# Mamba-2 and differential attention trunk: chunk products issued as two column halves, rows scaled by 1/rms once, and a fixed order of instructions up to there

## The chip, the cores and the metric

The kernel runs on one core of one Trainium2 chip. Its time is the device time of one execution in microseconds (us). The core has five engines that run side by side, each with its own queue: TensorE (PE: matmuls and transposes through the array; its weight loads are listed as PEld), VectorE (DVE), ScalarE (ACT), GpSimd (POOL) and SyncE (SP, which issues most DMAs here). Matmul results go to PSUM, eight banks of 128 x 512 float32; everything else lies in SBUF.

## The reference

One sequence of 512 tokens with 1024 features goes through two layers and a last RMSNorm. Layer 0 is a Mamba-2 mixer, layer 1 a differential attention over keys and values that are projected once from the output of layer 0. The change lies almost wholly in layer 0, so only that is shown:

```
h = rms_norm(x, norm_g)                 # x * (1/rms of the row) * gain
zxbcdt = h @ w_in                       # z: 2048, xbc: 4096, dt: 32 columns
xbc = silu(causal_depthwise_conv(xbc, conv_w, conv_b))   # 4 taps along the tokens
dt = softplus(dt_raw + dt_bias); a = -exp(a_log)
# state-space scan in chunks, per group (8) and head (4 a group):
y_diag = einsum("blsgr,bsgrp->blgrp", cb[..., None] * decay, x_c)   # within a chunk
y_off  = einsum("blgn,bgrpn->blgrp", c_c, state) * exp(acs)         # from earlier chunks
y = y_diag + y_off + d_skip * xs
y = gated_group_rms_norm(y, z, gate_norm_g)
x = x + y @ w_out
```

The kernel takes chunks of 128 tokens, so there are four. The 1/rms of a row is one number a token; it commutes with the projection, and so it can be applied to the rows of x, or to the outcome of the projection.

## The kernel before, in words

**Precision.** Every large product is made of three float32r matmuls: both operands are split into a head and a remainder (`hh`/`hl` for rows, `whi`/`wlo` for weights), and `mm3` (line 227) adds head x head, head x remainder and remainder x head into one bank. A head is written by ACT (a copy that rounds), the remainder by DVE (value minus head). The weights come in blocks of 1 MB (`load`, line 122), each split in four or eight pieces by `head` and `rest` (lines 137 and 143), with the norm's gain multiplied in. The small products of the scan are plain float32, which leaves two records of weight load and two of matmul for each product.

**The start (lines 351 to 450).** x is loaded twice: transposed (`xt`, four tiles of two 128-feature slices) and by tokens (`x_tok`). `split_x` makes `hh` and `hl` from the unscaled transposed rows. The gate projection z0 has four banks `pz0`, one for each tile of 128 tokens; its first half uses slices 0 to 3 of the rows, the second half slices 4 to 7. ACT squares `x_tok` to get the row sums, `rsqrt` (line 233) makes 1/rms as a column `r_col`, and `scales` (line 294) turns it into a row: POOL writes four diagonal matrices, a matmul with ones spreads them over the partitions (`aps_r`), and ACT copies the outcome to SBUF as `r_row`. Meanwhile PE makes `ps_dt`, the dt columns, with small weights `dw`. From `ps_dt` come `pre`, the softplus, the cumulated decays `acs`, which go to DRAM and come back spread over partitions for `decays` (line 532).

**Where 1/rms is applied before.** The rows are never scaled. The gate takes `r_col` as the scale of its SiLU (`z_out`, line 344). Each of the 32 outputs of the group projections is multiplied by `r_row` in PSUM in `conv` (line 477) ahead of the four taps. `pre` is multiplied by its part of the row (line 411).

**The dense stream.** `stream_a` (line 521) yields the large projections one after another in the order `z0 g0 g1 z1 g2 g3 z2 g4 o0 g5 z3 g6 g7 o1 o2 o3`: z for the gate, g for a group's B, C and two x tiles, o for the output projection. `ssd(g)` (line 552) is emitted when group g is through. In it, `pyd` (lines 600 to 607) is the product within a chunk: for each of two halves q of the sequence one bank, in it two chunks times four heads, each `dec[:, h, c, :]` (128 x 128, stationary) against `xdt[:, c, h, :]` (128 x 64, moving). DVE then adds the bank to `dx`.

**What sets the order.** The framework's scheduler orders instructions on each engine from a planned timeline, in which earlier emission has precedence. Where `V.on`, `A.on` or `T.on` is true (class `Ordered`, line 43), the instructions of that engine keep the order in which they are written. Before, this holds for DVE and ACT in the first four slices, and for PE, DVE and ACT from the end of the Mamba layer on in parts.

**The end (lines 902 to 1053).** The output projection of the attention runs in pieces (tile t, column half n, heads hs). For tiles 2 and 3, `add_in` (line 941) adds the residual to the bank in PSUM before its last matmuls, `gate_head` (line 850) makes the rows `oh` (head, ACT) and `ol` (remainder, DVE) for those matmuls, and `square_in`, `last_root` and `scale` do the last norm.

Of the kernel before, what the change touches and what calls it, by code (L numbers as in the profile page):

```python
# [61 lines left out]
def trunk(ctx, tc, x, x_t, par, w_dt, w_in, w_out, w_kvqg, w_bo, d_skip, lam_qk, fin_g, out):  # L62
# [59 lines left out]
    def load(i):  # L122

        seg = segs[i]
        src, gains = source(seg)
        nk = 8 if seg[0] in "vkqt" else 4
        w = 2048 // nk
        raw = wp.tile([P, nk, w], F32, tag="raw", name=f"raw{i}", bufs=2)
        fetched[0] += 1

        def split():

            pool, tags = (bp, ("dec", "dec")) if seg == ("o", 3, 1) else (wp, ("whi", "wlo"))
            hi, lo = (pool.tile([P, nk, w], F32R, tag=tag, name=f"{n}{i}", bufs=2) for n, tag in zip(("whi", "wlo"), tags))
            ready[seg] = (hi, lo)

            def head(k):
                if gains:
                    A.activation(hi[:, k, :], raw[:, k, :], AF.Copy, scale=gains[k])
                else:  # L140
                    A.copy(hi[:, k, :], raw[:, k, :])

            def rest(k):
                if gains:
                    V.scalar_tensor_tensor(out=lo[:, k, :], in0=raw[:, k, :], scalar=gains[k],
                                           in1=hi[:, k, :].bitcast(F32), op0=ALU.mult, op1=ALU.subtract)
                else:
                    V.tensor_tensor(out=lo[:, k, :], in0=raw[:, k, :], in1=hi[:, k, :].bitcast(F32), op=ALU.subtract)

            return [(head, rest, k) for k in range(nk)]  # L150

        if i == 0:

            nc.sync.dma_start(raw[:, 0, :], src[:, 0:w])
            for n in range(2):
                nc.sync.dma_start(xt[0][:, 0, n * 256:(n + 1) * 256], x_t[:, 0, n * 256:(n + 1) * 256])
            nc.sync.dma_start(raw[:, 1, :], src[:, w:2 * w])
            nc.sync.dma_start(xt[0][:, 1, :], x_t[:, 1, :])
            for k in range(2, 4):
                nc.sync.dma_start(raw[:, k, :], src[:, k * w:(k + 1) * w])  # L160
                nc.sync.dma_start(xt[1][:, k - 2, :], x_t[:, k, :])
            for i in range(2, 4):
                nc.sync.dma_start(xt[i], x_t[:, 2 * i:2 * i + 2, :])
            nc.sync.dma_start(prc[:], par[:, C_CB:N_PAR])
        else:
            nc.sync.dma_start(raw.rearrange("p k n -> p (k n)"), src)
        return split
# [102 lines left out]
    def run(gen):  # L270
        for _ in gen:
            pass
# [12 lines left out]

    def squares(ss, t, sq=None):
        if sq is None:  # L290
            sq = small.tile([P, D], F32, tag="wide", name=f"sq{t}", bufs=2)
        A.activation(sq, x_tok[:, t, :], AF.Square, accum_out=ss[:, t:t + 1])

    def scales(tag, ss):

        V.tensor_scalar(out=ss, in0=ss, scalar1=ROOT2 / D, scalar2=ROOT2 * EPS, op0=ALU.mult, op1=ALU.add)
        col = res.tile([P, NT], F32, tag="r_col", name=f"{tag}r_col")
        V.tensor_copy(col, rsqrt(ss, NT, "y"))
        w = small.tile([P, NT + 1, P], F32, tag="wide", name=f"{tag}diag", bufs=2)
        GP.memset(w[:, NT], 1.0)  # L300
        for t in range(NT):
            GP.tensor_tensor(out=w[:, t], in0=ident, in1=col[:, t:t + 1].to_broadcast([P, P]), op=ALU.mult)
        ps = long_bank(f"{tag}ps_r")
        T.matmul(ps, lhsT=w[:, NT], rhs=w[:, 0:NT].rearrange("p t n -> p (t n)"), start=True, stop=True)
        row = res.tile([P, S], F32, tag="r_row", name=f"{tag}r_row")
        A.copy(row, ps)
        return col, row

    def turn_rows(tag, t, xn, hh, hl):
# [33 lines left out]

    def z_out(j, t, ps):
        zs = bp2.tile([P, 512], F32, tag="zs", name=f"zs{j}_{t}", bufs=6)
        A.activation(zs, ps, AF.Silu, scale=r_col[:, t:t + 1])
        zt[j, t] = zs


# [10 lines left out]

    begin = small.tile([P, 1], F32, name="begin", bufs=1)
    A.activation(begin, ident[:, 0:1], AF.Copy)
    first = load(0)()
    wh, wl = ready.pop(("z", 0, 0))
    pz0 = [mm_bank(f"pz0_{t}") for t in range(NT)]
    V.on = A.on = True
    for k in range(4):
        lay(first[k])
        for n in (slice(0, 256), slice(256, S)) if k == 0 else (slice(0, S),):
            split_x(k, n)  # L370
    V.on = A.on = False
    for k in range(4):
        for t in range(NT):
            tk = slice(t * P, (t + 1) * P)
            mm3(pz0[t], (hh[:, k, tk], hl[:, k, tk]), (wh[:, k, :], wl[:, k, :]), k == 0, False)
    for k in range(4, KD):
        split_x(k)
    fetch(2)
    for t in range(NT):
        nc.sync.dma_start(x_tok[:, t, :], x[t * P:(t + 1) * P, :])  # L380
    ss = sm.tile([P, NT], F32, name="ass")
    for t in range(NT):
        squares(ss, t)
    r_col, r_row = scales("a", ss)
    V.tensor_scalar(out=sg1, in0=prm[:, C_SG:C_SG + 1], scalar1=0.5 * (1.0 - LAM0), scalar2=None, op0=ALU.mult)
    dtw_raw = sm.tile([P, KD, H], F32, name="dtw_raw")
    nc.sync.dma_start(dtw_raw[:], w_dt)

# [9 lines left out]
    for k in range(KD):  # L398
        w = dw[:, k].rearrange("p a b h -> p (a b h)")
        T.matmul(ps_dt, lhsT=w, rhs=hh[:, k, :], start=k == 0, stop=False)  # L400
        T.matmul(ps_dt, lhsT=w, rhs=hl[:, k, :], start=False, stop=k == KD - 1)

    pre = sm.tile([P, P], F32, name="pre")
    for c in range(NQ):
        sl, hi, lo = (slice(i * H, (i + 1) * H) for i in (c, 0, 1))
        cs = slice(c * P, (c + 1) * P)
        A.copy(pre[sl, :], ps_dt[lo, cs])
        V.tensor_tensor(out=pre[sl, :], in0=ps_dt[hi, cs], in1=pre[sl, :], op=ALU.add)
# [3 lines left out]
    V.tensor_scalar(out=pre, in0=pre, scalar1=prm[:, C_DTB:C_DTB + 1], scalar2=None, op0=ALU.add)  # L412
    e1 = sm.tile([P, P], F32, name="e1")
    A.activation(e1, pre, AF.Abs)
    A.activation(e1, e1, AF.Exp, scale=-1.0)
# [28 lines left out]
    nc.sync.dma_start(dsk[:], d_skip.partition_broadcast(P))  # L444


    w0 = use(("z", 0, 1))
    for t in range(NT):
        run(tok_mm(pz0[t], t, 1, w0))
        z_out(0, t, pz0[t])  # L450
# [20 lines left out]
    def conv(ps, ft, name, bufs):  # L471
        xc = bp2.tile([P, S], F32, tag=f"xc_{name}", name=f"xc{ft}", bufs=bufs)
        at = C_CW - C_CB + 4 * ft
        cw = [prc[:, at + k:at + k + 1] for k in range(4)]

        u = ps
        V.tensor_tensor(out=u, in0=ps, in1=r_row, op=ALU.mult)
        A.activation(xc, u, AF.Identity, scale=cw[3], bias=prc[:, ft:ft + 1])
        for k in (2, 1, 0):
            d = 3 - k  # L480
            V.scalar_tensor_tensor(out=xc[:, d:], in0=u[:, :S - d], scalar=cw[k], in1=xc[:, d:], op0=ALU.mult, op1=ALU.add)
        A.activation(xc, xc, AF.Silu)
        return xc

# [67 lines left out]
    def ssd(g):  # L552
# [349 lines left out]
    def rows():  # L902
        ws = {0: use_b(("c", 2, 0), 1, 2)}
        for t, n, hs in ((0, 0, (4, 5)), (1, 0, (4, 5)), (0, 1, (4, 5)), (1, 1, (4, 5)),
# [214 lines left out]
```

## Time and profile before

| what | value |
|---|---|
| median of 3 runs | 736.55 us (736.23 to 737.25) |
| the profiled execution | 736.51 us |
| its span on the core | 734.7 us |
| mean granted TensorE clock | 0.998 |
| HBM read and written | 68.02 MB and 2.16 MB, 96 GB/s over the span |
| chain that ended last | PE 86%, DVE 6%, ACT 5% |

The span is what the trace covers; the execution's time is 1.8 us longer. In the page, a line of the first part gives an engine's busy time, its share and its instructions; the slices cut the span in 40 equal parts and give the busy share in tenths. A group's row names the tile that is written, the tiles that are read, the shape, the count, the summed busy time and the mean of one in ns. In the wait view a row names who waited for whom, the sum, how often, and the longest. In the timeline a row starts with the start and the length in us. Nearly all lines say L53, since a helper issues them, so they are told apart by the tiles' names.

### The profile page before, as it was taken

What the parts mean: (1) busy time and instruction counts of PE and PEld (TensorE: products, weight loads), DVE (VectorE), ACT (ScalarE), POOL (GpSimd) and SP (SyncE); (2) the same over time, 40 slices, a digit from 0 to 9 for tenths busy, and PEclk for the clock granted to TensorE, in tenths of its full rate; (3) what the DMA queues carried; (4) which work ended last, traced back from release to release, by engine and by line L of the source; (5) the groups of instructions that cost most, each with busy time, mean ns of one, the idle gap of its engine ahead of it and who ended that gap; (6) DMA issues with size and microseconds to landing.
All of it is one profiled execution on the core that took longest, in us unless ns stands there. A gap on an engine that the chain in (4) does not pass through costs nothing.

```text
span 734.7 us, 10327 instructions
## 1 busy us (share of the span) xinstructions
PE 723.1 (98%) x3733; PEld 605.0 (82%) x3733; DVE 530.8 (72%) x1202; ACT 445.3 (61%) x975; POOL 114.8 (16%) x158
## 2 busy tenths in 40 slices
PE   9999999999999999999999999999999999999996
PEld 7788878888887888877888879888898898889874
DVE  5679955798568669469895655666757857785886
ACT  6849672864829356256433258766766766766566
POOL 0117231402233141150110201000000000000002
PEclk9999999999999999999999999999999999999999
DMA  8552313224132233132113220331221131122003
GB/s 314 215 193 97 128 45 116 78 95 172 59 114 65 108 115 116 58 116 102 71 58 114 87 86 8 115 115 58 65 109 57 58 116 58 58 80 93 29 1 114
DMA packets 12914, 70.83 MB, mean 96 GB/s; under 512 B 1728, under 2 KB 2496, under 8 KB 5312
## 3 DMA queue, kind: packets, MB, share of 16 engines
q1 hardware_dynamic: 12576, 69.90, 26.5%
q8 instruction: 29, 0.48, 0.3%
q10 hardware_dynamic: 288, 0.28, 0.1%
q14 instruction: 21, 0.17, 0.1%
HBM read 68.02 MB, written 2.16 MB: 96 GB/s over the span
## 4 chain that ended last, share of the span: by engine, by line
PE 86%; DVE 6%; ACT 5%; issue 1%; DMA 1%; POOL 0%; ACTq 0%; POOLq 0%; SPq 0%
PE pg L53 20%; PE po L53 13%; PE pz L53 10%; PE pt L53 7%; PE pv L53 6%; PE pq L53 6%; PE pk L53 6%; PE pyd L53 4%; PE pb L53 3%; PE sc L53 3%; PE pc L53 2%; DVE wlo L53 2%; ACT L53 1%; PE pyt L53 1%; PE pxt L53 1%
## 5 line engine op out<-in xcount | busy, mean ns | idle before, releaser
L53 DVE SCALAR_TENSOR_TENSOR wlo<-raw,prm,whi 128x512 fp32r<-128x512 f32 (+1 forms) x256 | 151.4, 640 | 49.6 <-ACT whi L53 49.2
L53 ACT ACTIVATE whi<-raw,prm 128x512 fp32r<-128x512 f32 (+1 forms) x256 | 137.1, 609 | 58.5 <-PE pz L53 12.4
L53 PE MATMUL pg<-a_hi,whi 128*128 128x512 f32 x256 | 102.4, 401 | 0.4 <-DVE xc L53 0.4
L53 PE MATMUL pg<-a_hi,wlo 128*128 128x512 f32 x256 | 102.7, 404 | 0.0
L53 PE MATMUL pg<-a_lo,whi 128*128 128x512 f32 x256 | 101.4, 397 | 0.0
L53 DVE SCALAR_TENSOR_TENSOR xc<-pg,prc,xc 128x511 f32<-128x511 f32 (+2 forms) x96 | 70.0, 743 | 4.4 <-ACT xc L53 3.6
L53 PEld LDWEIGHTS pg<-a_hi,whi 128*128 128x128 f32 x256 | 48.2, 188 | 11.4 <-issue 0.8
L53 PEld LDWEIGHTS pg<-a_hi,wlo 128*128 128x128 f32 x256 | 48.1, 188 | 11.0
L53 PEld LDWEIGHTS pg<-a_lo,whi 128*128 128x128 f32 x256 | 48.2, 188 | 10.8
L53 PE MATMUL po<-whi,yh 128*128 128x512 f32 x128 | 50.9, 400 | 0.7 <-ACT yh L53 0.6
L53 PE MATMUL po<-wlo,yh 128*128 128x512 f32 x128 | 50.9, 400 | 0.4 <-DVE wlo L53 0.4
L53 PE MATMUL pz<-wlo,a_hi 128*128 128x512 f32 x128 | 50.5, 401 | 0.0
L53 PE MATMUL pz<-whi,a_lo 128*128 128x512 f32 x128 | 50.1, 399 | 0.0
L53 PE MATMUL po<-whi,yl 128*128 128x512 f32 x128 | 49.9, 396 | 0.0
L53 PE MATMUL pz<-whi,a_hi 128*128 128x512 f32 x128 | 49.6, 400 | 0.0
L53 ACT ACT_TABLE_LOAD x33 | 42.3, 1283 | 9.5 <-DVE xc L53 7.9
L957 POOL TENSOR_TENSOR ot<-ot,fg 128x512 f32<-128x512 f32 x4 | 5.1, 1285 | 257.6 <-PE pc L53 256.4
L53 ACT ACTIVATE s<-s,mx 128x128 f32<-128x128 f32 (+3 forms) x64 | 35.6, 559 | 9.5 <-DVE mx L53 9.3
L580 POOL TENSOR_TENSOR xe<-xdt,tok 128x256 f32<-128x256 f32 x24 | 15.4, 672 | 152.5 <-DVE xdt L53 152.5
L53 DVE CUSTOM_DVE_ANT_0 s<-sc,bias 128x128 f32<-128x128 f32 (+3 forms) x64 | 29.4, 488 | 12.3 <-PE sc L53 11.9
L53 PE MATMUL pv<-whi,b_hi 128*128 128x256 f32 x128 | 36.6, 286 | 0.0
L53 ACT ACTIVATE tmp<-dx 128x256 f32<-128x256 f32 x32 | 13.1, 411 | 38.0 <-DVE dx L53 38.0
(244 smaller groups left out, 1749.1 us busy)
## 6 DMA issues: line engine op xcount, KB each, us to landing
raw<-in_w_in SPq DMA_DIRECT2D x23, 1024.0 KB, 4.9
raw<-in_w_kvqg SPq DMA_DIRECT2D x16, 1024.0 KB, 4.8
dec<-acs_d SPq DMA_DIRECT2D x8, 1024.0 KB, 4.8
raw<-in_w_out SPq DMA_DIRECT2D x8, 1024.0 KB, 4.7
raw<-in_w_bo SPq DMA_DIRECT2D x4, 1024.0 KB, 4.8
x_tok<-in_x SPq DMA_DIRECT2D x4, 512.0 KB, 9.4
out<-ot SPq DMA_DIRECT2D x7, 256.0 KB, 2.4
raw<-in_w_in SPq DMA_DIRECT2D x4, 256.0 KB, 5.4
```

The source lines that it names most:

```text
L53: i = op(*args, **kw)
L580: GP.tensor_tensor(out=xe[:, c], in0=xdt[:, c], in1=toe_tok[:, c, hs].unsqueeze(2).to_broadcast([P, R, HD]), op=ALU.mult)
L957: GP.tensor_tensor(out=o, in0=o, in1=f, op=ALU.mult)
```

## The change

Five things are changed.

1. **Chunk products in halves** (`ssd`). Each `pyd` product becomes two, with columns 0 to 63 and 64 to 127 of `dec` as the stationary side, written to partitions 0 to 63 and 64 to 127 of the bank. The moving side is the same for both.
2. **Rows scaled once.** After the first projection, the row of 1/rms stays in PSUM and DVE multiplies the transposed rows `xt` by it, slice by slice (`scale_x`); ACT and DVE then write `hh` and `hl` anew in place (`head_x`, `rest_x`). z0 still uses `r_col`; the later gates use scale 1. `conv` loses its multiplication and reads the bank directly.
3. **Another `scales`.** The diagonals are written by DVE instead of POOL, the row's matmul is issued by a function that is called later, between the second and the third token tile of the second half of z0, and the copy to SBUF is gone.
4. **A fixed order** on PE, DVE and ACT from the start to the scaled rows. The dt weights are loaded early, in the place of the conv parameters `prc`, which go behind the third weight block; the second and third weight blocks are fetched at fixed places.
5. **Two residual additions at the end.** `add_in(2, 0)` is moved from the stream to behind `gate_head(h, 0, 2)`; `add_in(3, 1)` is moved into `gate_head(h, 3, 4)`, between the head and the remainder.

```diff
@@ load(0)
-            nc.sync.dma_start(prc[:], par[:, C_CB:N_PAR])
+            nc.sync.dma_start(dtw_raw[:], w_dt)
@@ scales
-        V.tensor_copy(col, rsqrt(ss, NT, "y"))
         w = small.tile([P, NT + 1, P], F32, tag="wide", name=f"{tag}diag", bufs=2)
         GP.memset(w[:, NT], 1.0)
+        V.tensor_copy(col, rsqrt(ss, NT, "y"))
         for t in range(NT):
-            GP.tensor_tensor(out=w[:, t], in0=ident, in1=col[:, t:t + 1].to_broadcast([P, P]), op=ALU.mult)
+            V.tensor_scalar(out=w[:, t], in0=ident, scalar1=col[:, t:t + 1], scalar2=None, op0=ALU.mult)
         ps = long_bank(f"{tag}ps_r")
-        T.matmul(ps, lhsT=w[:, NT], rhs=w[:, 0:NT].rearrange("p t n -> p (t n)"), start=True, stop=True)
-        row = res.tile([P, S], F32, tag="r_row", name=f"{tag}r_row")
-        A.copy(row, ps)
+        def row():
+            T.matmul(ps, lhsT=w[:, NT], rhs=w[:, 0:NT].rearrange("p t n -> p (t n)"), start=True, stop=True)
+            return ps
         return col, row
@@ z_out
-        A.activation(zs, ps, AF.Silu, scale=r_col[:, t:t + 1])
+        A.activation(zs, ps, AF.Silu, scale=1.0 if j else r_col[:, t:t + 1])
@@ start
-    V.on = A.on = False
+    T.on = True
...
-    fetch(2)
+    second = load(1)()
     for t in range(NT):
         nc.sync.dma_start(x_tok[:, t, :], x[t * P:(t + 1) * P, :])
-    ss = sm.tile([P, NT], F32, name="ass")
-    for t in range(NT):
-        squares(ss, t)
-    r_col, r_row = scales("a", ss)
...
+    third = load(2)()
+    nc.sync.dma_start(prc[:], par[:, C_CB:N_PAR])
@@ behind ps_dt
+    for piece in second:
+        lay(piece)
+    ss = sm.tile([P, NT], F32, name="ass")
+    for t in range(NT):
+        squares(ss, t)
     pre = sm.tile([P, P], F32, name="pre")
     for c in range(NQ):
...
+        A.copy(pre[c * H:(c + 1) * H, :], ps_dt[H:2 * H, c * P:(c + 1) * P])
+    r_col, row = scales("a", ss)
+    def scale_x(k):
+        V.tensor_tensor(out=xt[k // 2][:, k % 2, :], in0=xt[k // 2][:, k % 2, :], in1=r_row, op=ALU.mult)
+    def head_x(k):
+        A.copy(hh[:, k, :], xt[k // 2][:, k % 2, :])
+    def rest_x(k):
+        V.tensor_tensor(out=hl[:, k, :], in0=xt[k // 2][:, k % 2, :], in1=hh[:, k, :].bitcast(F32), op=ALU.subtract)
+    w0 = ready.pop(("z", 0, 1))
+    for t in range(2):
+        run(tok_mm(pz0[t], t, 1, w0))
+    r_row = row()
+    for t in range(2, NT):
+        run(tok_mm(pz0[t], t, 1, w0))
+    z_out(0, 0, pz0[0])
+    (h0, l0, _), (h1, l1, _), (h2, l2, _), (h3, l3, _) = third
+    h0(0), l0(0), h1(1)
+    scale_x(0), head_x(0), l1(1), scale_x(1)
+    h2(2), rest_x(0), z_out(0, 1, pz0[1])
+    head_x(1), scale_x(2), h3(3), rest_x(1)
+    head_x(2), l2(2), scale_x(3), z_out(0, 2, pz0[2])
+    head_x(3), rest_x(2), l3(3), rest_x(3), z_out(0, 3, pz0[3])
+    T.on = False
...
+    for k in range(4, KD):
+        scale_x(k)
+        head_x(k)
+        if k > 4:
+            rest_x(k - 1)
+    rest_x(KD - 1)
+    V.on = A.on = False
@@ conv
-        u = ps
-        V.tensor_tensor(out=u, in0=ps, in1=r_row, op=ALU.mult)
-        A.activation(xc, u, AF.Identity, scale=cw[3], bias=prc[:, ft:ft + 1])
+        A.activation(xc, ps, AF.Identity, scale=cw[3], bias=prc[:, ft:ft + 1])
@@ ssd
-                    T.matmul(pyd[q][:, o:o + HD], lhsT=dec[:, h, c, :], rhs=xdt[:, c, h, :], start=True, stop=True)
+                    for r in (slice(0, 64), slice(64, 128)):
+                        T.matmul(pyd[q][r, o:o + HD], lhsT=dec[:, h, c, r], rhs=xdt[:, c, h, :], start=True, stop=True)
@@ rows
-            elif (t, n, hs) == (2, 0, (6,)):
-                add_in(t, n)
@@ end
     gate_head(h, 0, 2)
+    until((2, 0, 6))
+    add_in(2, 0)
     turn(h, 2)
...
-    gate_head(h, 3, 4)
+    def between():
+        until((3, 1, 5))
+        add_in(3, 1)
+    gate_head(h, 3, 4, between)
     square_in(2, 1)
-    until((3, 1, 5))
     rest2 = last_root(2)
     scale(1, 0, r1)
-    add_in(3, 1)
```

More of the change, by code (lines that the diff above doesn't have):

```diff
@@ L362, in trunk @@
     A.activation(begin, ident[:, 0:1], AF.Copy)
+    dtw_raw = sm.tile([P, KD, H], F32, name="dtw_raw")
     first = load(0)()
@@ L377, in trunk @@
         split_x(k)
-    fetch(2)
+    second = load(1)()
     for t in range(NT):
         nc.sync.dma_start(x_tok[:, t, :], x[t * P:(t + 1) * P, :])
-    ss = sm.tile([P, NT], F32, name="ass")
-    for t in range(NT):
-        squares(ss, t)
-    r_col, r_row = scales("a", ss)
-    V.tensor_scalar(out=sg1, in0=prm[:, C_SG:C_SG + 1], scalar1=0.5 * (1.0 - LAM0), scalar2=None, op0=ALU.mult)
-    dtw_raw = sm.tile([P, KD, H], F32, name="dtw_raw")
-    nc.sync.dma_start(dtw_raw[:], w_dt)
+    third = load(2)()
+    nc.sync.dma_start(prc[:], par[:, C_CB:N_PAR])
     dw = bp2.tile([P, KD, 2, 2, H], F32R, tag="yh", name="dw", bufs=4)
@@ L401, in trunk @@
         T.matmul(ps_dt, lhsT=w, rhs=hl[:, k, :], start=False, stop=k == KD - 1)
+    for piece in second:
[3 more added lines that the diff above has]
+        squares(ss, t)
     pre = sm.tile([P, P], F32, name="pre")
     for c in range(NQ):
[L405 to L408, printed above, removed]
+        A.copy(pre[c * H:(c + 1) * H, :], ps_dt[H:2 * H, c * P:(c + 1) * P])
[21 more added lines that the diff above has]
+    T.on = False
+    for c in range(NQ):
+        sl = slice(c * H, (c + 1) * H)
+        V.tensor_tensor(out=pre[sl, :], in0=ps_dt[0:H, c * P:(c + 1) * P], in1=pre[sl, :], op=ALU.add)
     for c in range(NQ):
@@ L412, in trunk @@
     V.tensor_scalar(out=pre, in0=pre, scalar1=prm[:, C_DTB:C_DTB + 1], scalar2=None, op0=ALU.add)
+    for k in range(4, KD):
[5 more added lines that the diff above has]
+    V.on = A.on = False
+    V.tensor_scalar(out=sg1, in0=prm[:, C_SG:C_SG + 1], scalar1=0.5 * (1.0 - LAM0), scalar2=None, op0=ALU.mult)
     e1 = sm.tile([P, P], F32, name="e1")
@@ L444, in trunk @@
     nc.sync.dma_start(dsk[:], d_skip.partition_broadcast(P))
[L447 to L450, printed above, removed]
     ps_tt = ss_bank("ps_tt")
@@ L474, in conv @@
         cw = [prc[:, at + k:at + k + 1] for k in range(4)]
-        u = ps
-        V.tensor_tensor(out=u, in0=ps, in1=r_row, op=ALU.mult)
-        A.activation(xc, u, AF.Identity, scale=cw[3], bias=prc[:, ft:ft + 1])
+        A.activation(xc, ps, AF.Identity, scale=cw[3], bias=prc[:, ft:ft + 1])
         for k in (2, 1, 0):
             d = 3 - k
-            V.scalar_tensor_tensor(out=xc[:, d:], in0=u[:, :S - d], scalar=cw[k], in1=xc[:, d:], op0=ALU.mult, op1=ALU.add)
+            V.scalar_tensor_tensor(out=xc[:, d:], in0=ps[:, :S - d], scalar=cw[k], in1=xc[:, d:], op0=ALU.mult, op1=ALU.add)
         A.activation(xc, xc, AF.Silu)
```

## The prediction

> **What bounds the kernel now.** I read the page first: its head, its busy rows and its slices.
>
> ```profile
> span 734.7 us, 10327 instructions
> PE 723.1 (98%) x3733; PEld 605.0 (82%) x3733; DVE 530.8 (72%) x1202; ACT 445.3 (61%) x975; POOL 114.8 (16%) x158
> PE   9999999999999999999999999999999999999996
> ```
>
> TensorE (PE) is occupied in every slice but a part of the last. Occupied is not the same as fast, so the next view is who PE waits for.
>
> ```profile
> PE pyt L53 <- ACT tmp L53: 1.0, 2, 0.7
> PE po L53 <- ACT yh L53: 0.6, 1, 0.6
> PE pc L53 <- DVE pc L53: 0.4, 1, 0.4
> PE pc L53 <- DVE ol L53: 0.4, 1, 0.4
> ```
>
> These are its longest waits after the start, and they come to 2.4 us. So a DVE or ACT operation that is taken away gives almost nothing by itself: time comes off only if PE gets less to do, or if one of these waits goes. The next views are the products that the change splits, by tile and then in order of time on PE.
>
> ```profile
> L53 PEld LDWEIGHTS pyd<-xdt,dec x256: 187/192/192, 76.5 to 415.9; 128*128 128x128 f32 x128
> L53 PE MATMUL pyd<-xdt,dec x256: 217/275/275, 76.7 to 416.0; 128*128 128x64 f32 x128
> L53 DVE TENSOR_TENSOR dx<-pyd,dx x16: 680/682/692, 79.2 to 416.3; 128x512 f32<-128x512 f32 x16
> ```
>
> ```profile
> 75.80 0.59 PE L53 MATMUL psA<-xe,bt 128*128 128x256 f32 x2
> 76.23 0.59 PE L53 MATMUL psB<-xe,bt 128*128 128x256 f32 x2
> 76.67 1.89 PE L53 MATMUL pyd<-xdt,dec 128*128 128x64 f32 x16
> 78.37 0.48 PE L53 MATMUL pg<-a_hi,whi 128*128 128x512 f32 x1
> ```
>
> Each float32 product leaves two records (256 for 128 products). They stand in 16 blocks of 16 records, as many blocks as the DVE reads of their banks. A record's own duration (275 ns) overlaps its neighbours; what it costs is the distance to the next one. From 76.67 to 78.37 that is 1.70 us for 16 records, 0.106 each. Next to it psA, with 256 moving columns, takes 0.43 for two records, 0.215 each, or 0.84 ns a column. The 64 moving columns of pyd should then take 0.054. Twice that is paid, so what sets the distance here is not the moving side; what is left is the load of 128 stationary columns. All 16 blocks: 16 x 1.70 = 27.2 us, nearly 4% of the span, with no wait in it. That is the only sizeable PE work that the change touches.
>
> **The products in two halves.** 256 records become 512, each with 64 stationary columns. No row shows such a load; all in this kernel are 128x128. If a load takes time by its columns, it takes 0.053, as long as the 64 moving columns. Then a product has four records of about 0.054. One after the other they cost 8 x 4 x 0.054 = 1.73 a block: nothing gained, nothing lost. If the two halves, which use different columns of the array and different PSUM partitions, work beside each other, a block streams in 8 x 2 x 0.054 = 0.86 and saves 0.84, at most 13.4 us in all. Against this stands what it costs to go from whole to half arrays and back, twice a block. The nearest row is the record of 275 ns against its distance of 106: if the array must be empty at the change, up to 0.17 is exposed, and up to 0.19 more for a load (its row's 192 ns) that nothing hides. So two changes cost between 0 and 0.72 a block. I take 0.2, the low third: between psB and pyd, and between pyd and pg, the distances show no cost at all for another form of product, so the whole price must come from the change of shape alone. A block is then 0.86 + 0.20 = 1.06, and 16 x (1.70 - 1.06) = **10.2 us** saved; the ends are 13.4 saved and, with halves that take turns and both changes paid in full, 16 x 0.75 = 12.0 lost.
>
> The Trainium skill, "TensorEngine Tiling (Array Packing)", Key Properties, says that different tiles can load and multiply in parallel, which is the 0.86; the same list says that changing the tiling mode drains TensorE, which speaks against this change, since it asks for 32 such changes. No run here shows either. By the first rule alone the saving would be 13.4 us; with the second taken at its full bound it would be about 2 us.
>
> **The scaling.** The rows that price what goes and what comes:
>
> ```profile
> L53 DVE TENSOR_TENSOR pg<-pg,ar_row 128x512 f32<-128x512 f32 x32 | 22.1, 692 | 8.1 <-PE pg L53 7.9
> L53 DVE TENSOR_TENSOR a_lo<-xt,a_hi 128x512 fp32r<-128x512 f32 x7 | 4.6, 687 | 0.4 <-ACT a_hi L53 0.4
> L53 ACT CAST a_hi<-xt 128x512 fp32r<-128x512 f32 x7 | 4.2, 621 | 0.7 <-DMA xt<-in_x_t 0.6
> L53 ACT COPY ar_row<-aps_r 128x512 f32<-128x512 f32 x1 | 0.6, 590 | 0.0
> L302 POOL TENSOR_TENSOR adiag<-ident,ar_col 128x128 f32<-128x128 f32 x4 | 2.8, 740 | 3.9 <-DVE ar_col L53 3.9
> ```
>
> DVE loses the 32 multiplications in `conv`, 22.1 us spread over the group projections. It gains, all before about 45 us, eight scalings (0.69 each, priced by the same multiplication from PSUM), eight remainders (0.69) and four diagonals (0.23, by the 128x128 row quoted next): 5.5 + 5.5 + 0.9 = 11.9. ACT gains eight casts, 5.0, and loses the copy of the row, 0.6; POOL loses 2.8. The removed part lies beside PE work, and PE hardly waits for it: I count 0, and at best the 1.6 us of pyt and po waits. The added part lies on a path, because PE now needs scaled rows before the first group.
>
> ```profile
> 5.86 20.42 PE pz L53 x86
> 26.28 3.73 PE ps_dt L53 x16
> 30.01 0.46 PE pz L53 x2
> 30.47 0.86 PE aps_r L53 x2
> 31.33 1.86 PE pz L53 x8
> 33.19 14.69 PE pg L53 x63
> ```
>
> ```profile
> 16.01 2.57 ACT L53 ACTIVATE whi<-raw,prm 128x512 fp32r<-128x512 f32 x4 [1.61 <-DMA raw<-in_w_in]
> ...
> 22.55 0.19 ACT L53 ACTIVATION_READ_ACCUMULATOR sq<-x_tok 128x1 f32 x1
> 22.65 2.02 ACT L53 ACTIVATE dw<-dtw_raw,prm 128x64 fp32r<-128x64 f32 x8
> ...
> 22.78 0.17 DVE L53 TENSOR_SCALAR ass<-ass 128x4 f32<-128x4 f32 x1 [3.27 <-ACT sq L53]
> ...
> 25.59 0.17 DVE L53 COPY ar_col<-y_y 128x4 f32<-128x4 f32 x1
> ...
> 38.99 0.23 DVE L53 TENSOR_SCALAR q<-e 128x128 f32<-128x128 f32 x1 [1.52 <-ACT e L53]
> ```
>
> In the fixed order PE reaches the row's matmul after 48 + 16 + 24 others: 5.86 + 48 x 0.237 + 3.73 + 24 x 0.233 = 26.6. When is its operand there? ACT makes dw (2.0) first, from about 14.4, in the stretch where it had waited 1.6 for weights, so the four squares end at about 23.2 instead of 22.74. The chain on DVE took 3.0 (22.78 to 25.76) with dw's operations mixed in; without them 2.2 to 3.0. The diagonals take 4 x 0.23 on DVE instead of 2.8 on POOL. So 26.3 to 27.1: PE waits 0 to 0.5, and behind that matmul in its queue stand the last 24 products of the gate projection and the first group; I take 0.3. Then 24 products (5.6 us) run while DVE does four scalings, three remainders of weights and four of rows, 11 x 0.69 = 7.6, with some 1 us of handing over between DVE and ACT. The first group needs its fourth slice three products a slice later, 2.1 us: 8.6 us of need against 5.6 + 2.1 = 7.7 of cover, a wait of about 0.9. Before, this stretch (5.86 to 33.19, 114 records) lost 0.4. The start costs 0.3 + 0.9 - 0.4 = **+0.8 net** (0 to 2.5).
>
> Three things ride along. Slices 4 to 7 follow after nine small operations on pre (some 2.5) and eight of 0.69: done near 44, and first needed after 48 products of the first group, near 45; the cover is thin, and each microsecond late is one lost. The softplus chain, at 38.99 before, begins about 7 us later, and with it the first decays and the first pyd; PE has the second group and the second gate projection to run meanwhile, so 0. Of the DMAs, the 128 KB of dt weights go ahead of the second weight block where the 80 KB of prc stood; prc goes behind the third block and is first read by the first conv, tens of microseconds later. I cost both at 0; 48 KB more is about a twentieth of a 1 MB weight block.
>
> **The end.** Two additions move relative to the remainders that PE waits for.
>
> ```profile
> 712.26 0.70 DVE L53 TENSOR_TENSOR pc<-pc,x_tok 128x512 f32<-128x512 f32 x1
> ...
> 712.87 0.41 DVE L53 TENSOR_TENSOR ol<-pot,oh 128x256 fp32r<-128x256 f32 x1
> ...
> 713.34 0.50 PE L53 MATMUL pc<-whi,ol 128*128 128x512 f32 x1 [0.43 <-DVE ol L53]
> ```
>
> Here the addition stood ahead of the remainder; now it comes behind, and the 0.43 goes. The other wait, 0.4 for pc, is for the addition of the last tile, which now goes ahead of a remainder and fills DVE's wait for ACT. What is late next is the remainder behind it, needed three products (0.7) later, and it takes about 0.3: covered. Together **-0.8** (0 to -0.9).
>
> **The sum.** -10.2 + 0.8 - 0.8 = -10.2. The profiled execution took 736.51 (span 734.7 and 1.8 around it), the runs' median is 736.55: 726.3 from either.
>
> **The rivals.** *Forecast*: halves beside each other, cheap changes of shape (0 to 0.5 a block): 16 x 0.34 to 16 x 0.84 saved, 723 to 731; with the bounds of the start and the end 721 to 734. Chance 0.57. *Dear changes*: beside each other, but 0.5 to 0.72 a block for the changes: 2 to 5.5 saved, 731 to 735. For it speaks the 275 against 106, against it nothing. 0.13. *No overlap*: the halves take turns in one queue, as all records do here, and the changes are free: 1.73 a block, about 737. This is also the case in which the split does not do what it says. 0.13. *Slower*: the halves take turns and the array empties at each change; a block then lasts 1.73 plus 0.1 to 0.72, and 16 of them add 2 to 12 us: 738 to 749. (The drain that the Trainium skill names on the page and in the section above would be paid in this case and in the dear one.) It decides from the point where a block is longer than 1.70. If even a load of half the columns cost a full one, 0.106 for each of 32 records, it would be 27 more; nothing here excludes that, but a load whose time ignores its size is the farther reading of the rows. 0.12. *A wait at the start*: the saving is made, but PE stands 3 to 5 us behind the row or behind slices 4 to 7: 729 to 731. For it speaks the thin cover worked out above. 0.05.
>
> **The numbers.** 726.3. About 0.2%, 1.5 us, is what a measurement of this kernel tells from no change. Faster by more: 0.57 + 0.13 + 0.05 = 0.75. Within: most of the no-overlap case, 0.12. Slower: 0.12 and a rest of the no-overlap case, 0.13. The range 721 to 738 holds all but the slower case and a little at the low end.
>
> **What would show it.** In the profile after, the distance from a block's first pyd record to the next tile's: 1.06 right, 0.9 or 1.6 mis-sized, 1.7 no overlap, over 1.75 the slower rival. In the wait view, PE waiting for DVE in 26 to 36 us: under 1.5 in all. The first pyd near 84 instead of 76.67. No multiplication by ar_row in the conv rows, DVE's total lower by about 10. In the last 25 us, no wait for ol or pc. A PE total that falls by less than 4 us, or a new wait of over 2 us anywhere, would make the prediction wrong.

## The result, and the profile after

The changed kernel, called after below, takes 746.50 us (median of four runs, 745.75 to 749.18) against 736.59 us of the kernel before in the same comparison: ratio 1.0140 [1.0113, 1.0167], slower by 1.4% (the brackets hold the 95% interval of a ratio, here and below). The prediction was 726.3 us in a range from 721 to 738; the time lies outside it, and on the wrong side of the kernel before. The profiled execution took 745.75 us, its span on the core is 743.9 us, 9.2 more than before.

The head and the busy rows of the page after:

```profile
span 743.9 us, 10820 instructions
PE 719.7 (97%) x3989; PEld 594.7 (80%) x3989; DVE 530.3 (71%) x1190; ACT 447.2 (60%) x982; POOL 113.2 (15%) x154
PE   9997999999999898999999999999999999999995
```

PE's busy time fell by 3.4 us while the span grew by 9.2: PE now stands still for 12.6 us more. Three of its slices before the twentieth are below nine tenths. The wait view says for whom it stands:

```profile
PE pg L53 <- DVE xc L53: 5.4, 1, 5.4
PE pcb L53 <- ACT xc L53: 2.9, 1, 2.9
PE po L53 <- DVE x_tok L53: 2.7, 1, 2.7
...
PE pxt L53 <- DVE yl L53: 1.4, 1, 1.4
PE pc L53 <- DVE pc L53: 1.0, 1, 1.0
```

Before, the longest single wait behind the start was 0.7; the first five are longer than that. The split products themselves did nearly what was forecast. In order of time around the first block:

```profile
81.72 0.59 PE L53 MATMUL psB<-xe,bt 128*128 128x256 f32 x2
82.24 1.15 PE L53 MATMUL pyd<-xdt,dec 128*64 128x64 f32 x32
83.33 0.50 PE L53 MATMUL pg<-a_hi,wlo 128*128 128x512 f32 x1
```

32 records take 1.09 us, 0.034 each, where 16 took 1.70. The two records of psB ahead of them take 0.52 and not 0.44, so entering the half arrays costs 0.08 more. From psB to pg the piece is 1.61 long against 2.14: 0.53 saved, 16 x 0.53 = 8.5 us over the kernel (the 16 blocks of this trace differ by 0.02). This gain is in the 746.50, and over 18 us of loss must stand against it. The largest wait, in order of time on PE:

```profile
62.12 0.77 PE L53 MATMUL pg<-a_hi,whi 128*128 128x512 f32 x1 [5.35 <-DVE xc L53]
62.68 0.63 PE L53 MATMUL pg<-a_lo,whi 128*128 128x512 f32 x1
63.11 0.63 PE L53 MATMUL pg<-a_hi,wlo 128*128 128x512 f32 x1
...
65.24 0.40 PE L53 MATMUL pg<-a_lo,whi 128*128 128x512 f32 x1
```

The bank of a conv of the first group is to be reused, and DVE is not through with its taps. Behind the wait the products come every 0.43 us and not every 0.23 until 65.2. The stretch of ten microseconds from 60 gives the granted clock for that:

```profile
60.00:70.00 10.00, 7.88 (x31) 6.38 (x32) 7.73 (x11) 6.77 (x11) 7.66 (x11) 0.83 0.70 275
```

Behind the length of the stretch stand the busy times of PE, PEld, DVE, ACT and POOL with their counts, and then the clock: 0.83. The timeline of DVE shows what stands ahead of the taps and among them:

```profile
44.66 0.94 DVE L53 RECIPROCAL q<-q 128x128 f32<-128x128 f32 x1
...
47.47 1.41 DVE L53 SCALAR_TENSOR_TENSOR wlo<-raw,prm,whi 128x512 fp32r<-128x512 f32 x2
...
50.32 0.69 DVE L53 TENSOR_TENSOR a_lo<-xt,a_hi 128x512 fp32r<-128x512 f32 x1
...
54.44 0.42 DVE L53 TENSOR_TENSOR_SCAN acs<-ones,adt 128x128 f32<-128x128 f32 x1
56.00 0.75 DVE L53 SCALAR_TENSOR_TENSOR xc<-pg,prc,xc 128x511 f32<-128x511 f32 x1 [1.14 <-ACT xc L53]
...
61.22 0.75 DVE L53 SCALAR_TENSOR_TENSOR xc<-pg,prc,xc 128x509 f32<-128x509 f32 x1
```

The scheduler has put remainders of weights and steps of the softplus among the remainders of slices 4 to 7, so the last slice is ready at 51.0 and the cumulated decays (`acs`) at 54.9; before, the decays were there at 44.9. The first tap starts at 56.00; the first conv to be through has its third tap at 61.22, since taps of other convs and remainders of weights stand between, and PE goes on at 62.12.

### The profile page after: what moved, and what is told of

It reads as the page before. It is cut to its first block, busy times and chain, and to the rows that moved or that the text cites. A ratio compares the mean times of both kernels' runs of the same rounds, so it can differ in the third digit from the quotient of the medians.

```text
span 743.9 us, 10820 instructions
## 1 busy us (share of the span) xinstructions
PE 719.7 (97%) x3989; PEld 594.7 (80%) x3989; DVE 530.3 (71%) x1190; ACT 447.2 (60%) x982; POOL 113.2 (15%) x154
## 4 chain that ended last, share of the span: by engine, by line
PE 81%; DVE 11%; ACT 5%; issue 2%; POOL 1%; ACTq 0%; POOLq 0%
PE pg L53 16%; PE po L53 13%; PE pz L53 10%; PE pt L53 7%; PE pv L53 6%; PE pq L53 6%; PE pk L53 6%; DVE wlo L53 3%; PE pb L53 3%; PE sc L53 3%; PE pc L53 2%; PE pyd L53 2%; DVE xc L53 2%; ACT L53 2%; ACT tmp L53 1%
## 5 line engine op out<-in xcount | busy, mean ns | idle before, releaser
L53 DVE SCALAR_TENSOR_TENSOR wlo<-raw,prm,whi 128x512 fp32r<-128x512 f32 (+1 forms) x256 | 153.7, 648 | 39.9 <-ACT whi L53 39.5
L53 DVE SCALAR_TENSOR_TENSOR xc<-pg,prc,xc 128x510 f32<-128x510 f32 (+2 forms) x96 | 70.6, 745 | 18.2 <-ACT xc L53 17.5
L53 PE MATMUL po<-whi,yh 128*128 128x512 f32 x128 | 51.7, 404 | 3.3 <-DVE x_tok L53 2.7
L53 PE MATMUL pz<-whi,a_hi 128*128 128x512 f32 x128 | 52.5, 411 | 0.1
L53 PE MATMUL pz<-whi,a_lo 128*128 128x512 f32 x128 | 51.9, 406 | 0.0
L53 PE MATMUL pz<-wlo,a_hi 128*128 128x512 f32 x128 | 51.7, 404 | 0.0
L571 POOL TENSOR_TENSOR dec<-dec,tok 128x512 f32<-128x512 f32 x32 | 37.3, 1193 | 0.6
```

Source lines behind the costliest of these rows:

```text
L53: i = op(*args, **kw)
L571: GP.tensor_tensor(out=dec[:, h], in0=dec[:, h], in1=acs_tok[:, :, R * g + h].unsqueeze(2).to_broadcast([P, NQ, P]), op=ALU.subtract)
```

## The experiments

The first four kernels tell the parts of the change from each other, the next three the order of the instructions from the instructions themselves, one looks at the multiplication in `conv`, and the others at the longer start.

### The halves alone

```diff
 before, in ssd
-  T.matmul(pyd[q][:, o:o + HD], lhsT=dec[:, h, c, :], rhs=xdt[:, c, h, :], start=True, stop=True)
+  for r in (slice(0, 64), slice(64, 128)):
+      T.matmul(pyd[q][r, o:o + HD], lhsT=dec[:, h, c, r], rhs=xdt[:, c, h, :], start=True, stop=True)
```

> The kernel before, with nothing but the chunk products in two halves. Theory S (the loss of the change comes from the scaling and its fixed order at the start, and the halves are a clean gain): the 16 blocks shrink from 1.72 to 1.08 us and nothing new waits, so 736.5 - 10.2 = 726.3 us, 725 to 728. Theory H (the halves only let PE run into DVE and ACT earlier, and what they save comes back as new waits): 733 to 737 us, with new PE waits of 5 us or more.

744.43 us, ratio 1.0105 [1.0090, 1.0120], above the ranges of both theories. So the part that saves 8.5 us of PE work makes the kernel slower when it is made alone. Its wait view:

```profile
PE po L53 <- DVE x_tok L53: 6.7, 1, 6.7
PE pyt L53 <- ACT tmp L53: 1.8, 1, 1.8
```

No split product waits here. What differs is the order: up to the first pyd the instructions stand on every engine as before, and behind it, in the rest of the Mamba layer, DVE keeps fewer than half of its pairs of neighbours. The first that differs on DVE: `dx<-dx,zs` stands ahead of the next `pg<-pg,ar_row` before (80.79 and 81.12) and behind it here (81.98 and 81.39). The scheduler plans from durations that it reckons itself, and with other products it makes another plan.

### The rest without the halves

```diff
 after, in ssd
-  for r in (slice(0, 64), slice(64, 128)):
-      T.matmul(pyd[q][r, o:o + HD], lhsT=dec[:, h, c, r], rhs=xdt[:, c, h, :], start=True, stop=True)
+  T.matmul(pyd[q][:, o:o + HD], lhsT=dec[:, h, c, :], rhs=xdt[:, c, h, :], start=True, stop=True)
```

> The changed kernel, with the chunk products whole again. Theory S: all waits of the changed kernel stay and 16 x 0.64 us come back, 746.5 + 10 = 756.5 us, 754 to 759. Theory H: part of the waits after 100 us go as the blocks get longer, 746 to 750 us.

754.68 us, 1.0243 [1.0228, 1.0258], in the range of theory S. The scaled rows, the fixed order and the end, with the order that the scheduler makes for the rest, cost 18 us together. The halves, which lost 7.7 us in the kernel before, gain 7.6 us here, where the scheduler makes another plan again. The largest wait, 5.8 us of pg for xc, is the one that the changed kernel has.

### The end alone, and with the halves

```diff
 before, rows
-            elif (t, n, hs) == (2, 0, (6,)):
-                add_in(t, n)
 before, end
     gate_head(h, 0, 2)
+    until((2, 0, 6))
+    add_in(2, 0)
...
-    gate_head(h, 3, 4)
+    gate_head(h, 3, 4, between)
...
-    add_in(3, 1)
```

> The kernel before, with nothing but the two residual additions at the end moved. The prediction's step for it: 0.8 us less, 735.8 us. Rival, from the profile after, which shows PE waiting 1.0 us for the bank of the last tile and 0.5 for a head in the same place: the waits only change their names, 736.5 to 737.2 us.

738.42 us, 1.0015 [1.0005, 1.0025], 1.1 us more where the prediction's step was a gain of 0.8. Both waits of 0.4 are gone, and these have come in the timeline of PE:

```profile
713.50 0.50 PE L53 MATMUL pc<-whi,oh 128*128 128x512 f32 x1 [0.51 <-ACT oh L53]
...
724.83 0.50 PE L53 MATMUL pc<-whi,oh 128*128 128x512 f32 x1 [0.99 <-DVE pc L53]
```

With the halves beside it:

> The kernel before, with the halves and the moved additions, and no scaling of the rows. Theory S and the prediction's step for the end: 725.5 us. With the rival on the end: 726.3 to 727. Theory H: 733 to 737 us.

744.71 us, 1.0117 [1.0090, 1.0143], no different from the halves alone.

### Order and instructions apart

These three kernels are built twice. The order of the first build is kept as a list for each engine, and in the second each instruction is tied to the one ahead of it in that list, by an edge that orders and adds no semaphore. The second half of a product stands right behind the first.

```diff
+def pin(tc, order):
...
+    for places in order["engines"].values():
+        last = None
+        for at in places:
+            i = first[at]
+            for i in (i, behind[i.name]) if i.name in behind else (i,):
+                if last is not None:
+                    tc.add_manual_dep(i, last.name, dep, reason="pin")
+                last = i
```

The control, the kernel before in its own order:

> Control: the kernel before, built twice; the second build is held, instruction by instruction on every engine, to the order that the first one got. Both theories: 736.6 us, the kernel before again, 735.8 to 737.5.

737.64 us, 1.0003 [0.9993, 1.0012]. The ties cost nothing that shows, and the trace has the instructions in the order of before on every engine. The halves in the order of before:

> The products in halves, with every other instruction of every engine held to the order of the kernel before. Theory O (what lost the gain is the new order that the scheduler writes once the products look different to it; on the chip the halves cost what was predicted): 736.5 - 10.2 = 726.3 us, at most 2 us of new waits, 725 to 729. Theory H (DVE and ACT cannot follow a PE that is 10 us ahead, whatever the order): 733 to 744 us.

730.70 us, 0.9911 [0.9895, 0.9928]: this beats both kernels, though it lies between the ranges of the two theories. Its rows (a helper has line 78 here) around the same block, and its waits:

```profile
77.29 0.59 PE L78 MATMUL psB<-xe,bt 128*128 128x256 f32 x2
77.82 1.15 PE L78 MATMUL pyd<-xdt,dec 128*64 128x64 f32 x32
78.90 0.50 PE L78 MATMUL pg<-a_hi,whi 128*128 128x512 f32 x1
```

```profile
PE pyt L78 <- ACT tmp L78: 1.3, 3, 0.7
PE po L78 <- DVE wlo L78: 1.0, 1, 1.0
PE po L78 <- ACT yh L78: 0.6, 1, 0.6
```

Again 1.61 us from psB to pg; no long wait. And the reverse, whole products in the order that the halves alone had got:

> The opposite: whole products, with every instruction held to the order that the scheduler wrote for the halves alone (e1_halves, 744.4 us). Theory O: the waits belong to the order and stay, and 10 us of PE come back, 754 us, 750 to 756. Theory H: the waits were made by the early PE and go with it, 737 to 745 us.

751.07 us, 1.0182 [1.0166, 1.0197], in the range of theory O, with the waits of that order:

```profile
PE po L78 <- DVE x_tok L78: 6.8, 1, 6.8
PE pyt L78 <- ACT tmp L78: 2.0, 2, 1.9
```

The products are those of the kernel before, and yet it is 13 us slower. In either order the halves are worth the same within the uncertainty: from 1.0003 to 0.9911 in the one, from 1.0182 to 1.0105 in the other, 6.8 and 5.7 us. The theory that the halves bring nothing in any order (an earlier PE running into late operands) is out. The order is what costs.

### The wait for the first conv

After's order was kept but for five instructions, which should have brought the first taps ahead of the softplus:

```diff
 after, held to its own order
+    ahead("Activation", mark["ident"], mark["toe"])
+    ahead("DVE", mark["taps"], mark["dtp"])
```

> The changed kernel, held to its own order but for two moves: on ACT the first operation of the first two convs stands ahead of the exponential that waits for the softplus chain, and on DVE the three taps of the first conv stand ahead of the chain's last three operations. Theory Q (the 5.4 us wait at 56 us is made by convs that stand in the queues behind the softplus chain, which the scaling made 10 us later): the wait and the slowed clock behind it go, 746.5 - 6.5 = 740 us, 738 to 742. Rival (DVE has too much to do there in any order): the wait moves to the next bank, 745 to 747 us.

749.51 us, 1.0162 [1.0146, 1.0177]. Above both ranges; its view has

```profile
PE pbt L78 <- ACT xc L78: 3.1, 1, 3.1
...
PE ps_tt L78 <- DVE dtp L78: 2.0, 1, 2.0
```

The wait of 5.4 for that bank is gone: the three taps now stand together and end at 58.0, and PE goes on with pg at 59.58 instead of 62.12. But PE now waits 2.0 for the end of the softplus chain and 3.1 for the SiLU of the first conv, each with the slow products behind it, and the kernel isn't faster. The theory fell: the convs begin hardly earlier (54.85 and not 55.21), since their banks are not full earlier. In after's order PE works on the four banks of the first group in turn, so all four end close together near 56, where before the first was full at 48.

### The longer start with before's order behind it

All of the change but the end; up to the last rescaled remainder the order is after's, behind it before's. The order lies in the kernel as a list of numbers; here and in the last two kernels the edit of the list is given in words.

```diff
 after, with the end of before
+    each engine: as after, up to rest_x(KD - 1); then as before, of what is left
```

> All of the change but the two moved additions at the end. The instructions up to the last rescaled remainder stand as the kernel after has them; every instruction behind them, on all engines, is held to the order of the kernel before (without the 32 multiplications, which are gone; the products in halves at the places of the whole ones). Theory O (what was lost is the order of the rest): the start costs about what the prediction said, +0.8, or up to 2 more where products of the first group wait for slices 4 to 7; beside the 730.70 us of the halves in the order of before that gives 731 to 734 us, and the wait of 5.4 us for the first conv with the slow clock behind it is gone. Rival S (the longer start by itself is dear, whatever the order behind it: the remainders come late, the first conv with them, and the decays 7 us later): 737 to 742 us, with PE waits of 3 us or more between 40 and 85 us.

736.85 us, 0.9982 [0.9971, 0.9993]. The time lies between the two ranges, and both theories have a part. The scheduler's own order behind the start costs, with the end, the difference to after, 1.0140 - 0.9982, or 11.6 us. It isn't lost where the wait of 5.4 stands: counted in order of time, PE's 1000th record starts at 195.4 here and at 194.7 in after, and its 1600th at 302.3 and 310.1. Between these two places after has its waits of 1.4 (207.7), 2.7 (244.3) and 2.9 us (296.1) and, behind the last, 1.5 us of slow products: 8.5 us, which is what the 1600th record has fallen back against the 1000th. But 736.85 is not 731 to 734, and the waits say why (the helper's line is 228):

```profile
PE ps_tt L228 <- DVE dtp L228: 3.7, 1, 3.7
...
PE pbt L228 <- ACT xc L228: 1.2, 1, 1.2
PE pxt L228 <- ACT xc L228: 1.0, 1, 1.0
```

```profile
41.40 1.46 DVE L228 TENSOR_TENSOR a_lo<-xt,a_hi 128x512 fp32r<-128x512 f32 x2
...
51.72 0.29 DVE L228 SCALAR_TENSOR_TENSOR dtp<-pre,pl 128x128 f32<-128x128 f32 x1
```

The slices are ready at 42.9, and PE doesn't wait for them. dtp comes at 51.7, 8 us later than before (43.77), and PE's transpose of it stands where it had stood; on ACT the second conv and the SiLU of the first stand behind an exponential (`een`) that needs the decays from DRAM.

### The multiplication in conv alone

This kernel leaves the scaling of the group projections out, and so it computes something else; it serves for the time alone.

```diff
 before, halves, order of before, in conv
-        V.tensor_tensor(out=u, in0=ps, in1=r_row, op=ALU.mult)
```

> The kernel before with the halves, held to the order of before, and with the 32 multiplications in conv left out (the group projections are then not scaled by 1/rms at all, and nothing takes their place). It measures alone what the 22 us of DVE work are worth. The prediction's step (beside PE work, so 0): 729.7 to 731.2 us, as with them (730.70). Rival (DVE's share bounds the scan: the waits that PE has left in that order, 4.2 us in all, are DVE and ACT operations behind these multiplications): 727 to 729 us.

727.28 us, 0.9857 [0.9835, 0.9879]. Against the halves with it (0.9911) that is 0.0054, 4.0 us give or take 2.0. The rival was right. The waits that are left:

```profile
PE pyt L227 <- ACT tmp L227: 1.0, 2, 0.6
PE po L227 <- ACT yh L227: 0.6, 1, 0.6
```

The 1.0 for wlo and the 0.4 for xc are gone. This kernel and the one before it differ by the start: 0.9982 - 0.9857 is 9.2 us, give or take 1.8. The traces show where it goes. With the longer start ACT has the same operations in the same order, all later by 8.3 to 8.5 us: `toe` at 52.90 and not 44.60, `een` at 62.32 and not 53.80, the first SiLU at 64.51 and not 55.98; and the first pyd stands at 85.70 and not 77.19. So the softplus chain is 8.3 us late, and PE is 8.5 us late at the first pyd; from there to the end its records stay 8.5 to 9.0 us later.

### Can another order hide the longer start?

```diff
 the longer start, order of before, edited in group 0
+    PE: the three ps_tt behind 24 more products
+    ACT: four convs ahead of een and dec
+    DVE: first taps ahead of wlo; second taps behind tok
```

> The kernel of the run before (start of the change, then the order of before; 736.85 us) with one thing moved: in group 0 the work that needs the late softplus chain stands behind the work that doesn't. PE's three transposes of the decays come 24 products later; ACT's four convs come ahead of the two exponentials of the decays; DVE's taps of the first conv come ahead of the weight remainders that had stood there, and those of the second follow the token-wise copy. Theory L (the start's cost is only that the softplus chain, 8 us later, stands ahead of the convs in that order; PE has other work, if the order lets it have it): the waits of 3.7, 1.2 and 1.0 us and the slow clock at 50 to 60 us go, 728 to 732 us. Rival D (the added scalings, casts and remainders themselves load DVE and ACT up to 45 us, or the later decays delay the scan whatever stands ahead of them): 735 to 738 us, with waits of the same size at other places between 45 and 90 us.

734.08 us, 0.9950 [0.9932, 0.9969]: less than with the unmoved order, but between the two ranges. One wait has taken the place of three, and the clock falls again:

```profile
63.10 0.90 PE L228 MATMUL pbt<-ident,xc 128*128 128x128 f32 x3 [4.04 <-ACT xc L228]
63.66 0.78 PE L228 MATMUL pg<-a_hi,wlo 128*128 128x512 f32 x1
64.23 0.63 PE L228 MATMUL pg<-a_hi,whi 128*128 128x512 f32 x1
64.66 0.63 PE L228 MATMUL pg<-a_lo,whi 128*128 128x512 f32 x1
...
68.04 0.40 PE L228 MATMUL pg<-a_hi,whi 128*128 128x512 f32 x1
```

```diff
 the same
+    ACT: the SiLU of the first conv ahead of four weight heads
```

> The kernel of the run before (734.08 us) with one more operation moved: the SiLU of the first conv stands ahead of four weight heads on ACT, and not behind them and the fourth conv. There PE waited 4.0 us for the three transposes of that conv, and the products behind the wait came every 0.43 us instead of 0.233 until 67.6, another 2.0. Theory L (the longer start costs nothing where the order gives PE other work): both go, 728 to 729.5 us, within 2 of the 727.3 us that the halves give in the order of before without the scaling and without the longer start. Rival D (the late decays or the busier DVE still hold PE): 732 us or more, with a wait of over 2 us at another place before 100 us.

732.88 us, 0.9949 [0.9931, 0.9967]. The wait of 4.0 and the slow clock went, and the span fell from 732.4 to 730.8, but against its own runs of the kernel before the ratio is the same, so this last move isn't shown to gain. Theory L is not confirmed: 0.0092, 6.8 us, still lie between it and the kernel without the longer start. They are no longer in one place:

```profile
PE pyt L228 <- ACT tmp L228: 2.0, 3, 1.3
...
PE pg L228 <- DVE xc L228: 1.0, 1, 1.0
```

```profile
60.00:70.00 10.00, 8.99 (x44) 6.89 (x43) 9.89 (x12) 5.42 (x8) 8.03 (x10) 1.00 0.77 296
70.00:80.00 10.00, 9.68 (x43) 7.28 (x42) 6.22 (x11) 8.56 (x13) 8.96 (x12) 1.00 0.12 51
...
90.00:100.00 10.00, 10.00 (x48) 8.20 (x47) 10.00 (x16) 4.57 (x9) 7.07 (x8) 1.00 0.54 198
```

The first pyd is at 80.89, 3.7 behind the kernel without the longer start. DVE (the third busy time) is full from 60 to 70 and from 90 to 100, but not between; and without the longer start it is as full from 60 to 70 (9.93), where PE has no such waits. So a full DVE isn't shown to be the cause. Whether a better order by hand would hide the rest stays open.

## Why the prediction was wrong, point by point

The runs split the difference into four steps, each the difference of two ratios times 736.6 us:

| step | from, to | us |
|---|---|---|
| halves, order of before | 1.0003, 0.9911 | -6.8 (1.4 either way) |
| conv without the multiplication, order of before | 0.9911, 0.9857 | -4.0 (2.0) |
| rows scaled in the start, order of before behind it | 0.9857, 0.9982 | +9.2 (1.8) |
| the scheduler's own order, and the end | 0.9982, 1.0140 | +11.6 (2.1) |

**The halves, -10.2.** The mechanism was right: a block lasts 1.09, 1.06 was forecast. The term was mis-sized, since the entry costs 0.08 more ahead of the block, where the prediction didn't look, and since 1.7 of the 8.5 us don't arrive: 0.6 is the wait of po for wlo (0.4 in the control, 1.0 with the halves), and the rest is no more than the uncertainty (1.4). The Trainium skill, "TensorEngine Tiling (Array Packing)", Key Properties, says that tiles work in parallel and that a change of mode drains TensorE. The first agrees with the traces here: 32 records in 1.09 us can't have streamed one after the other at 0.054 each. Of the second no row shows the drain itself; beyond 0.86 of streaming some 0.3 is left for two changes of shape with what surrounds them, well under the bound of 0.72.

**DVE's 22 us, "I count 0".** Wrong by 4.0 (2.0 to 6.0). Of the wait view of before, 1.6 us was taken as the most that could go; two rows of the same view were not counted:

```profile
PE po L53 <- DVE wlo L53: 0.4, 1, 0.4
PE pg L53 <- DVE xc L53: 0.4, 1, 0.4
```

With the halves these waits are 1.0 and 0.4, and these two go when the multiplications go, with 0.3 of those for pyt. Between the two profiles the span falls by 3.6 (729.0 to 725.4) and the waits in the view by 1.7 (4.1 to 2.4, without that of the start). Where the other 1.9 lie isn't shown; single executions of one kernel here differ by as much. The sign "DVE's total lower by about 10" did not show either, 530.8 to 530.3. With the order held, DVE's busy time falls from 532.5 to 514.2 without the multiplications, and the longer start brings it back to 525.0.

**The start, +0.8.** The steps that were priced came out: the row's matmul ran at 27.42 without a wait, the first pg at 33.87 (33.03 in the profile of before, 33.78 in that of the control, which starts with the same instructions), and with before's order the slices were ready at 42.9 against "near 44". The step that failed is the sentence on the softplus chain: "PE has the second group and the second gate projection to run meanwhile, so 0". The chain is 8 us later, as was said, but the other work did not run meanwhile. With before's order behind the start, products that needed nothing of the chain stood behind ps_tt, which waited 3.7 us, convs stood on ACT behind an exponential of the decays, and the first pyd came 8.5 us later. In after's own order it is the wait of 5.4 for the taps, with the slow products behind it: PE's 300th record starts at 75.7 in after, at 77.4 with before's order, and at 68.8 without the longer start. The start cost 9.2 where 0.8 was said, and the moves in group 0 recovered 2.4 of it (0.9982 to 0.9949). What holds the rest isn't shown.

**The end, -0.8.** 1.1 us the other way (0.4 to 1.8). The addition was moved off one wait, and the head `oh` (0.5) and the addition of the last tile (1.0) are late instead. "What is late next is the remainder behind it" was the step, and it looked only at the remainder.

**What no step of the sum held.** All terms were made against the order of the trace of before, as if the rest stayed where it was. Only the start is written out by hand; behind it a planner decides up to the end of the Mamba layer, and 11.6 us went there and in the end. It is the largest term, and no rival named it. The slower rival had the sign for another reason: it decided from a block longer than 1.70, and the block is 1.09. The last sentence of the prediction had the right alarms: PE's total fell by 3.4, less than 4, and of new waits over 2 us there are three.

How the 11.6 us divide is shown in part: the end measured 1.1, and the waits for yl, x_tok and xc between 207 and 297 us, with the slow products behind the last, come to 8.5. That the order makes these three waits follows from the run that has none of them; what in the order makes each was not tested. The wait of 5.4 belongs to the step above it, the longer start.

## What to carry to other kernels

Where a scheduler makes the order, a change to one product is two changes, and they have to be timed apart: hold every other instruction to the old order, and the halves are worth 6.8 us; let the plan be made anew, and the same edit loses 7.7 in one kernel and gains 7.6 in the other. When a chain of small operations moves later, ask of each engine which instruction in its queue needs the chain and what stands behind it: here PE and ACT stood still with work behind it that didn't need the chain. And DVE work that PE rarely waits for is not free: here 0 was counted and 4.0 us came (2.0 to 6.0), of which the wait view accounts for 1.7.

## What the runs showed of the hardware that was not expected

A wait can cost PE more than its length. After 5.35 us of standing still, the 512-column products came every 0.43 us from 62.7 to 65.2, and not every 0.23; after 4.04 us, from 64.2 to 67.6. In the changed kernel it also happens behind a shorter wait, and goes on to 300.7:

```profile
296.11 1.16 PE L53 MATMUL pcb<-xc,xc 128*128 128x128 f32 x8 [2.94 <-ACT xc L53]
297.33 0.62 PE L53 MATMUL pz<-whi,a_hi 128*128 128x512 f32 x1
297.75 0.63 PE L53 MATMUL pz<-wlo,a_hi 128*128 128x512 f32 x1
```

In the kernel with the halves alone it happens behind 1.24 us, at 293.38, until 296.9. But after a wait of 2.65 us, in the changed kernel at 244.31, the record that follows had its usual 0.50:

```profile
244.31 0.50 PE L53 MATMUL po<-whi,yh 128*128 128x512 f32 x1 [2.65 <-DVE x_tok L53]
```

And in the kernel held to after's order but for five instructions nothing follows the same 2.94 us (at 299.38). So the length of one wait doesn't decide; what does isn't shown here.

The Trainium skill, "TensorE: Matmul & The Clock Gate", Part 1, says that the clock is halved after an idle window of about 3.4 us, and gives 426.7 ns from start to start for 512 columns then. The distances here agree. The waits of 2.94 and 1.24 us are shorter than that window, and there the measurement decides. A slow stretch, where it comes, costs 1.5 to 2 us on top of the wait: an estimate from the four above, with seven to ten distances each of 0.43 for 0.23.
